# Moving the SBUF start addresses of split weights and moving activations in a two-block transformer kernel

## The chip, the core and the metric

The program runs on one core of one Trainium2 chip. The metric is the device time of one execution in microseconds (us); the time of a version is the median of its runs. In what follows PE is TensorE, PEld its weight loads, DVE is VectorE, ACT is ScalarE, POOL is GpSimd and SP is SyncE.

## The reference

Two transformer stages over 256 tokens of width 1024, all in fp32: a first block of two layers, then a second block of one layer.

```python
for l in range(2):                                  # first block
    h = rmsnorm(x, norm_mix[l]); proj = h @ w_in[l]
    # 12 slices: q, k, v, index heads, recurrence q/f/i/g, two gates
    y_attn = dsa_attention(...)                     # top-64 keys per query
    o = hgrn2_chunked(...)                          # gated linear recurrence
    merged = sigmoid(ga) * (y_attn @ w_proj_attn[l]) + sigmoid(gb) * (y_hgrn @ w_proj_hgrn[l])
    x = x + merged @ w_out[l]
    g, u = split(rmsnorm(x, norm_ffn[l]) @ w_ffn_in[l])
    x = x + (silu(g) * u) @ w_ffn_out[l]
...                                                 # second block: modulated norm, forgetting
                                                    # attention + depthwise conv, w_o, one more ffn
```

Nearly all the arithmetic is in the products with weights: 352 weight tiles of 128 x 1024 numbers.

## The kernel before

**Products in three parts.** Each weight tile arrives by DMA as fp32 in a tile `raw` (4 buffers). `do_split` (L720) makes two fp32r tiles of it: ACT writes the rounded half `wH`, DVE subtracts and writes the rest `wL` (6 buffers of 4096 bytes per partition for each). Activations are split in the same way into a high and a low tile. `mm3` (L781) then issues three matmuls for each product, and PE loads 128 columns of weights for each:

```python
PE.matmul(o, wH, xH, ...)      # stationary wH, moving xH
PE.matmul(o, wH, xL, ...)
PE.matmul(o, wL, xH, ...)
```

The first operand is the stationary one (loaded into the array), the second moves through it, 256 columns at a time. In what follows a "feature" matmul is one of these: stationary weights, 128 x 256 moving activations.

**The moving activations live in four kinds of tiles.** `xH`, `xL` (`act_pair`, L873) hold the normed input of a layer part; they feed `pair_mm` (L786), which is most of the kernel. `E` tiles hold the merged branches for `w_out`. The `t512` tiles (shown as `t` in the profile) hold the halves of the ffn's middle activation for `out_mm` (L896). The `b4` tiles (shown as `b`) hold the two branch outputs for `proj_mm` (L795). In the second block `token_mm`, `out_tm` and `first_tm` swap the roles: activations are stationary and 512 columns of `wH` or `wL` move. An output in PSUM is called `mm` or `side`.

**Where a tile starts.** A pool lays its buffers one behind another in every partition. `act_pair` makes its two tiles 128 elements longer than needed and starts the data `PLACE` = 28 elements (112 bytes) into them. `GAP` is a filler in the pool of constants, so that the pool of weights starts at a multiple of 512 bytes.

**What sets the order.** The program records every instruction, and `Recorder.issue` (L428) simulates the engines with estimated costs and emits the instructions in the order that it found. A `Buf` with a `tag` takes one of `bufs` places; which physical buffer it gets is left to the pool. In the first and second layer's ffn, runs of `pair_mm` matmuls alternate with runs of `out_mm` matmuls.

Of the kernel before, what the change touches and what calls it, by code (L numbers as in the profile page):

```python
# [15 lines left out]
F32 = mybir.dt.float32  # L16
F32R = mybir.dt.float32r
# [10 lines left out]
FF, NJ = 2816, 11  # L28
LINE = 128

GAP = 64

PLACE = 28
OUT_SHAPE = [256, 1024]
EPS = 1e-6
NEG = -1e30
# [208 lines left out]
class Buf:  # L245


    def __init__(self, pool, shape, dtype, name, tag, bufs, space):
        self.pool, self.shape, self.dtype, self.name, self.tag, self.bufs, self.space = pool, shape, dtype, name, tag, bufs, space
        n = int(np.prod(shape[1:]))  # L250
        self.writer = np.full(n, -1)
        self.readers = []
        self.group = [-1]
        self.ops = 0
        self.tile = None
        self.slot = None
        self.seq = None
        self.number = None
        self.read = {}

    def real(self):
        if self.tile is None:
            kw = {"tag": self.tag, "bufs": self.bufs} if self.tag else {}
            self.tile = self.pool.tile(self.shape, self.dtype, name=self.name, **kw)
        return self.tile
# [84 lines left out]
class Recorder:  # L350
# [77 lines left out]
    def issue(self):  # L428
# [25 lines left out]
        slots, waiting, first, line = {}, {}, {}, {}  # L454
        for op in ops:
            for b in op.bufs:
                if b.tag and b.seq is None:
                    slots.setdefault(b.tag, [0.0] * b.bufs)
                    b.seq = len(line.setdefault(b.tag, []))
                    line[b.tag].append(b)  # L460
                    first[b.tag] = 0
# [16 lines left out]
        while len(order) < len(ops):  # L478

            best = None  # L480
            for e in names:
                if avail[e]:
                    t = free_at[e]
                elif pending[e]:
                    t = max(free_at[e], pending[e][0][0])
# [6 lines left out]
            t, e = best  # L492
            while pending[e] and pending[e][0][0] <= t:
                _, _, op = heapq.heappop(pending[e])
                heapq.heappush(avail[e], (-op.urgency, op.index, op))
            op, skipped = None, []
            while avail[e]:
                item = max(avail[e], key=prio) if e in "VS" else avail[e][0]
                avail[e].remove(item)
                heapq.heapify(avail[e])  # L500
                cand = item[2]

                later, taken, turn = 0.0, {}, {}
                for b in sorted((b for b in cand.bufs if b.tag and b.slot is None), key=lambda b: b.seq):
                    s, n = slots[b.tag], taken.get(b.tag, 0)
                    f = turn.get(b.tag, first[b.tag])
                    jump = b.seq - f
                    ahead, reserve = JUMP.get(b.tag, (0, 0))
                    if len(s) <= n or (jump and (jump > ahead or len(s) - n <= reserve)):
                        later = None  # L510
                        waiting.setdefault(b.tag, []).append(cand)
                        break
                    later = max(later, sorted(s)[n])
                    taken[b.tag] = n + 1
                    if not jump:
                        f += 1
                        while f < len(line[b.tag]) and line[b.tag][f].slot:
                            f += 1
                        turn[b.tag] = f
                if later is not None:  # L520

                    for b in cand.bufs:
                        if b.space == "PSUM":
                            later = max([later] + [end + hop(x, e) for x, end in b.read.items() if x != e])
                            x = "S" if e == "V" else "V"
                            if e in "VS" and YIELD and free_at[x] <= t and any(
                                    p[0] <= t and p[2].urgency > cand.urgency and b in p[2].bufs for p in pending[x]):
                                later = max(later, t + 50.0)
                later = None if later is None else later if later > t else 0.0
                if later is None:  # L530
                    continue
                if later:
                    cand.ready = later
                    push(cand)
                    continue
                if e == "S" and TABLES.get(cand.func) and not (TABLES[cand.func] & tables):

                    other = [a for a in avail[e] if a[0] < item[0] + 4000.0 and (not TABLES.get(a[2].func) or TABLES[a[2].func] & tables)]
                    if other:
                        skipped.append(item)  # L540
                        continue
                op = cand
                break
# [29 lines left out]
            done = op.end + (LOAD_LATENCY if e == "DMA" else 0.0)  # L573
            order.append(op)
            for b in op.bufs:
                if b.space == "PSUM":
                    b.read[e] = op.end
                if b.tag and b.slot is None:
                    heapq.heappop(slots[b.tag])
                    b.slot = True  # L580
                    q, old = line[b.tag], first[b.tag]
                    while first[b.tag] < len(q) and q[first[b.tag]].slot:
                        first[b.tag] += 1
                    if first[b.tag] != old:
                        for w in waiting.pop(b.tag, []):
                            w.ready = max(w.ready, t)
                            push(w)
                if e == "PE" and b.number is not None:
                    at = max(at, b.number)
                b.ops -= 1  # L590
                if b.ops == 0 and b.tag:
                    heapq.heappush(slots[b.tag], done + 200.0)
                    for w in waiting.pop(b.tag, []):
                        w.ready = max(w.ready, done + 200.0)
                        push(w)
# [24 lines left out]
def program(tc, I, out, pw, cw, tap=None, stop=None):  # L620
# [11 lines left out]
    with es:  # L632
        es.enter_context(tc.manual_schedule())
        const = es.enter_context(tc.tile_pool(name="const", bufs=1))
        wp = es.enter_context(tc.tile_pool(name="wp", bufs=3))
        act = es.enter_context(tc.tile_pool(name="act", bufs=1))
# [4 lines left out]
        def body():  # L641
            uid = [0]

            def new(pool, shape, dt=F32, tag=None, bufs=None):
                n = int(np.prod(shape[1:]))
                line = LINE if dt == U8 else LINE // 4
                if pool is not psum and pool is not dram and n % line:

                    v = new(pool, [shape[0], -(-n // line) * line], dt, tag, bufs)[:, :n]
                    return v if len(shape) == 2 else v.rearrange("p (a b) -> p a b", a=shape[1])  # L650
                uid[0] += 1
                b = Buf(pool, shape, dt, f"{tag or 'c'}_{uid[0]}", tag, bufs or 1, "PSUM" if pool is psum else "SBUF")
                return View(b, np.arange(n).reshape([1] + list(shape[1:])), shape[0], ())
# [48 lines left out]
            NT = I["W"].shape[0]  # L702
            raw, split = {}, {}
            N_RAW, N_SPLIT = 4, 6

            halves = slice(0, 512), slice(512, 1024)

# [12 lines left out]
            def do_split(i):  # L720
                if i < NT and i not in split:
                    load(i)
                    H = new(wp, [128, 1024], F32R, tag="wH", bufs=N_SPLIT)
                    L = new(wp, [128, 1024], F32R, tag="wL", bufs=N_SPLIT)
                    R.feed = i
                    for c in cuts(i) if i < CUT or i not in HALVES else halves:
                        A(H[:, c], raw[i][:, c], AF.Copy)
                        tt(L[:, c], raw[i][:, c], H[:, c].bitcast(F32), OP.subtract)
                    R.feed, H.buf.number = None, i
                    split[i] = (H, L)  # L730

# [139 lines left out]
                return v, r, rstd  # L871

            def act_pair():  # L873
                return tuple(new(act, [128, 2048 + 128], F32R, tag=t, bufs=1)[:, PLACE:PLACE + 2048].rearrange("p (a b) -> p a b", a=8)
                             for t in ("xH", "xL"))

            def scaled_split(g, acc=None):

# [127 lines left out]
            def layer(l, first, X):  # L1006
                R.bias = NORM_BIAS if first else 0.0
                ms, rt, rstd = norm_x()
                R.bias = 0.0
                em, rtok = new(act, [128, 2], F32, tag="em"), new(act, [128, 2], F32, tag="rtok")  # L1010
                ts(em, ms, EPS, None, OP.mult)
                V.tensor_copy(rtok, rt)
                tap(f"rstd{l}", rstd)
# [45 lines left out]
                for t in range(2):  # L1059
                    n = 128 * (t + 1)  # L1060
# [27 lines left out]
                for p in range(2):  # L1088
# [12 lines left out]
                    if l == 1:  # L1101
                        for b in range(2):
                            h = 2 * p + b
                            s = slice(b * 256, b * 256 + 256)
# [39 lines left out]
                for c in range(4):  # L1144
                    for t in range(2):
                        o = (c % 2) * 256 + t * 128
# [65 lines left out]
                for lev in range(8):  # L1212
# [3 lines left out]
                    elif lev < 7:  # L1216
# [9 lines left out]
                        n = 64 // m  # L1226
                        for j in range(8):
                            t, h = divmod(j, 4)
                            for b in range(n):
                                o = h * 256 + t * 128 + 2 * m * b  # L1230
# [19 lines left out]
                    if lev < 6:  # L1250
                        n = 512 // m
                        o = 0 if lev == 0 else 512 - 2 * n
# [461 lines left out]
```

## Time and profile before

| what | value |
|---|---|
| time, median of 3 runs | 1131.16 us (1129.42 to 1132.87) |
| the profiled execution: its time, its span | 1129.97 us, 1128.2 us |
| PE busy, share of the span, matmuls | 1097.2 us, 97%, 9388 |
| PE weight loads busy | 1034.5 us, 92% |
| DVE busy | 857.5 us, 76% |
| ACT busy | 595.5 us, 53% |
| mean granted clock of PE | 0.992 of 2.4 GHz |

The span runs from the first to the last instruction in the trace. A matmul's duration in the trace is its latency (about 280 ns for a feature matmul), and consecutive matmuls overlap; how fast PE works is read from the distance between the starts of consecutive matmuls, called the pitch here.

### The profile page before, as it was taken

Reading aid. Unit: us, or ns where it says so; the run is one execution under the profiler, and the core shown is the slowest. Engines: PE = TensorE matmul, PEld = TensorE weight load, DVE = VectorE, ACT = ScalarE, POOL = GpSimd, SP = SyncE. Lnnn points to the kernel's source line nnn. Section 1 sums busy time; section 2 is a strip of 40 time slices with the busy share of each in tenths; the row PEclk is TensorE's granted clock in tenths of the full one; section 3 lists DMA queues with packets and bytes.
Section 4 is the critical chain, followed back from the end, with each engine's and each line's share of the span. In section 5 each row is a group of like instructions: output and inputs, shape, how many; then the busy total and the mean of one; then the engine's idle time right before and its main releaser. Section 6 shows DMA issues by size and latency. Waiting matters only on the chain.

```text
span 1128.2 us, 22970 instructions
## 1 busy us (share of the span) xinstructions
PE 1097.2 (97%) x9388; PEld 1034.5 (92%) x9388; DVE 857.5 (76%) x1590; ACT 595.5 (53%) x905; POOL 7.2 (1%) x16
## 2 busy tenths in 40 slices
PE   6999999999999999999999999999899989999996
PEld 6988999999999999888999999999798578999995
DVE  7999976899966589998676998756879668554554
ACT  6744694644444467446744544444754665443442
POOL 1000000000000000000000000000000000000000
PEclk9999999999999999999999999999999999999998
DMA  7553534689956543643345899655457225556550
GB/s 263 186 180 111 197 123 169 207 314 337 335 190 217 189 154 117 210 146 133 132 172 196 288 346 334 218 201 195 145 176 201 95 76 184 175 186 219 189 169 37
DMA packets 59992, 217.47 MB, mean 193 GB/s; under 512 B 6872, under 2 KB 10096, under 8 KB 56816
## 3 DMA queue, kind: packets, MB, share of 16 engines
q1 hardware_dynamic: 59888, 216.02, 55.8%
q8 instruction: 73, 1.20, 0.4%
q14 instruction: 31, 0.25, 0.1%
HBM read 214.19 MB, written 1.63 MB: 191 GB/s over the span
## 4 chain that ended last, share of the span: by engine, by line
PE 89%; DVE 6%; ACT 3%; issue 1%; DMA 1%; SPq 0%; DVEq 0%; ACTq 0%
PE mm L400 60%; PE side L400 29%; ACT t L400 2%; DVE t L400 1%; DVE b L400 1%; DVE wL L400 1%; DMA raw<-in_W 1%; DVE small L400 1%; ACT wH L400 1%; ACT L604 0%; DVE c L400 0%; DVE xL L400 0%; DVE AC L400 0%; SPq L400 0%; DVE sc L400 0%
## 5 line engine op out<-in xcount | busy, mean ns | idle before, releaser
L400 ACT ACTIVATE wH<-raw 128x1024 fp32r<-128x1024 f32 (+1 forms) x390 | 369.0, 968 | 400.5 <-PE mm L400 221.1
L400 DVE TENSOR_TENSOR wL<-raw,wH 128x1024 fp32r<-128x1024 f32 (+1 forms) x390 | 425.6, 1112 | 151.3 <-ACT wH L400 149.4
L400 PE MATMUL mm<-xH,wH 128*128 128x256 f32 x1760 | 486.8, 279 | 9.2 <-ACT wH L400 9.2
L400 PE MATMUL mm<-xH,wL 128*128 128x256 f32 x1760 | 488.3, 280 | 0.8 <-DVE wL L400 0.8
L400 PE MATMUL mm<-xL,wH 128*128 128x256 f32 x1760 | 488.5, 279 | 0.5 <-DVE xL L400 0.5
L400 PEld LDWEIGHTS mm<-xH,wH 128*128 128x128 f32 x1760 | 330.6, 189 | 11.7 <-ACT wH L400 9.2
L400 PEld LDWEIGHTS mm<-xL,wH 128*128 128x128 f32 x1760 | 331.2, 189 | 3.4 <-issue 0.9
L400 PEld LDWEIGHTS mm<-xH,wL 128*128 128x128 f32 x1760 | 330.8, 189 | 3.5 <-DVE wL L400 1.7
L400 PE MATMUL side<-t,wH 128*128 128x256 f32 x704 | 127.6, 281 | 0.0
L400 PEld LDWEIGHTS side<-t,wH 128*128 128x128 f32 x704 | 108.2, 188 | 0.0
L400 PE MATMUL side<-t,wL 128*128 128x256 f32 x352 | 98.8, 281 | 0.0
L400 ACT ACTIVATE t<-t 128x512 f32<-128x512 f32 (+2 forms) x80 | 48.9, 620 | 39.8 <-DVE t L400 37.0
L400 PEld LDWEIGHTS side<-t,wL 128*128 128x128 f32 x352 | 66.2, 188 | 0.0
L400 DVE SCALAR_TENSOR_TENSOR E<-E,b 128x1024 f32<-128x1024 f32 x48 | 57.9, 1221 | 4.1 <-DMA E<-in_ada 3.9
L400 PE MATMUL side<-wH,t 128*128 128x512 f32 x176 | 57.3, 394 | 0.0
L400 DVE TENSOR_TENSOR t<-t,t 128x512 f32<-128x512 f32 (+2 forms) x78 | 53.1, 681 | 3.7 <-ACT t L400 2.9
L400 PE MATMUL mm<-b,wH 128*128 128x256 f32 x256 | 46.6, 283 | 0.0
L400 PE MATMUL side<-E,wH 128*128 128x256 f32 x256 | 46.4, 281 | 0.0
L400 DVE TENSOR_TENSOR t<-mm,rstd 128x512 f32<-128x512 f32 (+1 forms) x50 | 33.7, 678 | 14.4 <-PE mm L400 14.1
L400 PE MATMUL mm<-wH,xH 128*128 128x512 f32 x96 | 38.7, 412 | 1.9 <-ACT xH L400 1.9
L400 PEld LDWEIGHTS mm<-b,wH 128*128 128x128 f32 x256 | 39.9, 191 | 0.0
L400 PEld LDWEIGHTS side<-E,wH 128*128 128x128 f32 x256 | 39.3, 188 | 0.0
(205 smaller groups left out, 1198.7 us busy)
## 6 DMA issues: line engine op xcount, KB each, us to landing
raw<-in_W SPq DMA_DIRECT2D x348, 512.0 KB, 4.3
E<-in_ada SPq DMA_DIRECT2D x24, 1024.0 KB, 7.0
b<-c SPq DMA_DIRECT2D x16, 128.0 KB, 4.6
c<-in_xT SPq DMA_DIRECT2D x4, 256.0 KB, 5.1
raw<-in_W SPq DMA_DIRECT2D x4, 256.0 KB, 4.9
b<-in_c SPq DMA_DIRECT2D x2, 512.0 KB
out_y<-E SPq DMA_DIRECT2D x4, 256.0 KB, 2.0
c<-E SPq DMA_DIRECT2D x4, 143.0 KB, 3.4
```

The costliest lines, as they stand in the source:

```text
L400: op.emit = lambda: getattr(real, method)(*[get(a) for a in args], **{k: get(a) for k, a in kw.items()})
```

## The change

The six buffers of `wH` become six places in one ring tile, and those of `wL` likewise. A place's number comes from the scheduler (`heappop(slots[...])[1]`) instead of from the pool, and the data starts 100 elements (400 bytes) into the ring. `act_pair` uses plain tiles that start at the tile's start. A filler of 96 elements (`GAP_E`, behind `em`) moves all tiles that are laid out behind it by 384 bytes.

```diff
-PLACE = 28
+PLACE = 100
+GAP, GAP_E = 64, 96
...
     def real(self):
+        if self.ring is not None:
+            n = int(np.prod(self.shape[1:]))
+            o = PLACE + self.slot * n
+            return self.ring.real()[:, o:o + n]
...
-                    slots.setdefault(b.tag, [0.0] * b.bufs)
+                    slots.setdefault(b.tag, [(0.0, k) for k in range(b.bufs)])
...
-                    heapq.heappop(slots[b.tag])
-                    b.slot = True
+                    b.slot = heapq.heappop(slots[b.tag])[1]
...
+            def ring(tag):
+                if tag not in rings:
+                    rings[tag] = Buf(wp, [128, N_SPLIT * 1024 + 128], F32R, f"{tag}_ring", f"{tag}_ring", 1, "SBUF")
+                uid[0] += 1
+                b = Buf(wp, [128, 1024], F32R, f"{tag}_{uid[0]}", tag, N_SPLIT, "SBUF", rings[tag])
+                return View(b, np.arange(1024).reshape(1, 1024), 128, ())
...
-                    H = new(wp, [128, 1024], F32R, tag="wH", bufs=N_SPLIT)
-                    L = new(wp, [128, 1024], F32R, tag="wL", bufs=N_SPLIT)
+                    H, L = ring("wH"), ring("wL")
...
-                return tuple(new(act, [128, 2048 + 128], F32R, tag=t, bufs=1)[:, PLACE:PLACE + 2048].rearrange("p (a b) -> p a b", a=8)
-                             for t in ("xH", "xL"))
+                return (new(act, [128, 8, 256], F32R, tag="xH", bufs=1), new(act, [128, 8, 256], F32R, tag="xL", bufs=1))
...
-                em, rtok = new(act, [128, 2], F32, tag="em"), new(act, [128, 2], F32, tag="rtok")
+                em, rtok = new(act, [128, 2 + GAP_E], F32, tag="em")[:, :2], new(act, [128, 2], F32, tag="rtok")
```

What the operands of the feature matmuls start at, as bytes past a multiple of 512 in a partition (every slice of 128 weight columns or 256 activation columns in a tile keeps the tile's value):

```text
tile                before   after     moving minus weights, modulo 512: before, after
wH, wL                   0     400
xH, xL  (pair_mm)      112       0     112   112
t512    (out_mm)       128       0     128   112
E       (w_out)        128       0     128   112
b4      (proj_mm)        0       0       0   112
```

On PE, at the place in the first layer's ffn where the first run of `out_mm` (moving `t512_526` and `t512_527`, output `side`) follows a run of `pair_mm` (moving `xH`, `xL`, output `mm`), there stood

```order
L400 MATMUL mm_536_3202<-xH_490_2951,wH_516_3129 128x256
L400 MATMUL mm_536_3202<-xL_491_2974,wH_516_3129 128x256
L400 MATMUL mm_536_3202<-xH_490_2951,wL_517_3156 128x256
L400 MATMUL side_504_3303<-t512_526_3217,wH_519_3144 128x256
L400 MATMUL side_504_3303<-t512_527_3229,wH_519_3144 128x256
L400 MATMUL side_504_3303<-t512_526_3217,wL_520_3189 128x256
```

and now stands

```order
L404 MATMUL mm_536_3060<-xH_490_2821,wH_ring_126 128x256
L404 MATMUL mm_536_3060<-xL_491_2844,wH_ring_126 128x256
L404 MATMUL mm_536_3060<-xH_490_2821,wL_ring_132 128x256
L404 MATMUL side_504_3156<-t512_526_3074,wH_ring_126 128x256
L404 MATMUL side_504_3156<-t512_527_3086,wH_ring_126 128x256
L404 MATMUL side_504_3156<-t512_526_3074,wL_ring_132 128x256
```

Nothing moved: the order of the instructions is the same on all five engines, and only the tiles' names and places differ.

On ACT, at weight tile 254 (the start of the second block, from which 38 tiles are split in two halves), the writes of `wH` with what each waits for (DMAHW is the landing of `raw`, PE the matmuls that read the place before) were

```order
L400 ACTIVATE wH_10042<-raw_9960 128x512 [waits DMAHW0_49,PE_49,Activation_49]
L400 ACTIVATE wH_10042<-raw_9960 128x512
L400 ACTIVATE wH_10090<-raw_9981 128x512 [waits DMAHW1_49,PE_49,Activation_49]
L400 ACTIVATE wH_10090<-raw_9981 128x512
L400 ACTIVATE wH_10117<-raw_10033 128x512 [waits DMAHW2_49,PE_49]
L400 ACTIVATE wH_10117<-raw_10033 128x512
```

and are

```order
L404 ACTIVATE wH_ring<-raw_9459 128x512 [waits DMAHW0_49,PE_49,Activation_49]
L404 ACTIVATE wH_ring<-raw_9459 128x512 [waits PE_49]
L404 ACTIVATE wH_ring<-raw_9479 128x512 [waits DMAHW1_49,PE_49,Activation_49]
L404 ACTIVATE wH_ring<-raw_9479 128x512 [waits PE_49]
L404 ACTIVATE wH_ring<-raw_9527 128x512 [waits DMAHW2_49]
L404 ACTIVATE wH_ring<-raw_9527 128x512 [waits PE_49]
```

Here a wait moved from the first half to the second: in a ring each half waits only for the matmuls that read that half. The second half waits for the same matmul that the whole tile waited for before, and the first half for one 12 to 24 matmuls earlier, or for none. For the tiles that are written in one piece the waits are unchanged.

## Rows read from the trace of the kernel before

**Rows 1.** The page, part 1: busy time of each engine.

```profile
PE 1097.2 (97%) x9388; PEld 1034.5 (92%) x9388; DVE 857.5 (76%) x1590; ACT 595.5 (53%) x905; POOL 7.2 (1%) x16
```

**Rows 2.** The page, part 4: the chain that ended last, by engine.

```profile
PE 89%; DVE 6%; ACT 3%; issue 1%; DMA 1%; SPq 0%; DVEq 0%; ACTq 0%
```

**Rows 3.** Waits of PE's matmuls: us in total, times, longest us.

```profile
PE mm L400 <- ACT wH L400: 9.2, 1, 9.2
...
PE mm L400 <- DVE wL L400: 0.8, 2, 0.5
```

**Rows 4.** Waits of all engines, same columns: the writes of the split weights.

```profile
ACT wH L400 <- PE mm L400: 221.1, 115, 5.3
...
ACT wH L400 <- DMA raw<-in_W: 36.9, 27, 5.9
```

**Rows 5.** Busy time by window, the two ffns of the first block.

```profile
core 0: us, PE busy (x) PEld busy (x) DVE busy (x) ACT busy (x) POOL busy (x), PEclk, DMA share, GB/s
245.00:407.00 162.00, 162.00 (x1399) 162.00 (x1399) 121.00 (x146) 73.66 (x83) 0.00 (x0) 1.00 0.72 254
643.00:813.00 170.00, 166.70 (x1437) 166.01 (x1435) 128.75 (x177) 79.64 (x99) 0.00 (x0) 1.00 0.71 249
```

**Rows 6.** Groups by line and form on PE: the feature matmuls and their counts.

```profile
L400 PE MATMUL mm<-xH,wH 128*128 128x256 f32 x1760 | 486.8, 279 | 9.2 <-ACT wH L400 9.2
L400 PE MATMUL side<-t,wH 128*128 128x256 f32 x704 | 127.6, 281 | 0.0
L400 PE MATMUL side<-t,wL 128*128 128x256 f32 x352 | 98.8, 281 | 0.0
L400 PE MATMUL mm<-b,wH 128*128 128x256 f32 x256 | 46.6, 283 | 0.0
L400 PE MATMUL side<-E,wH 128*128 128x256 f32 x256 | 46.4, 281 | 0.0
...
L400 PE MATMUL mm<-b,wL 128*128 128x256 f32 x128 | 36.0, 283 | 0.0
L400 PE MATMUL side<-E,wL 128*128 128x256 f32 x128 | 36.0, 281 | 0.0
```

**Rows 7.** Pieces of the chain that ended last: start us, us, what.

```profile
209.85 12.24 PE side L400 x103
...
365.70 3.08 PE side L400 x26
368.78 9.81 PE mm L400 x86
```

**Rows 8.** Timeline of PE: start us, us, what; starts at which the moving tile or the pitch changes.

```profile
170.69 0.28 PE L400 MATMUL mm<-b,wH 128*128 128x256 f32 x1
...
182.20 0.28 PE L400 MATMUL mm<-xL,wH 128*128 128x256 f32 x1
...
368.62 0.28 PE L400 MATMUL mm<-xH,wL 128*128 128x256 f32 x1
...
369.92 0.28 PE L400 MATMUL mm<-xL,wH 128*128 128x256 f32 x1
...
378.42 0.28 PE L400 MATMUL side<-t,wH 128*128 128x256 f32 x1
...
790.48 0.28 PE L400 MATMUL mm<-xL,wH 128*128 128x256 f32 x1
```

**Rows 9.** The same chain in the last ffn, where weights move, 512 columns each.

```profile
1040.55 2.78 PE side L400 x12
```

**Rows 10.** Groups by form on ACT: high halves written at 128 and 112 bytes past 512.

```profile
L400 ACT ACTIVATE t<-t 128x512 fp32r<-128x512 f32 x32 | 20.1, 628 | 27.4 <-DVE t L400 27.4
...
L400 ACT ACTIVATE xH<-t 128x512 fp32r<-128x512 f32 x8 | 5.0, 625 | 0.1
```

**Rows 11.** Groups by form on PE: fp32 transposes and matmuls of 128 columns.

```profile
L400 PE MATMUL side<-c,t 128*128 128x128 f32 x56 | 10.9, 277 | 0.2 <-DVE t L400 0.2
...
L400 PE MATMUL side<-c,c 128*128 128x128 f32 x32 | 4.2, 274 | 0.0
```

More of the change, by code (lines that the diff above doesn't have):

```diff
@@ L29 @@
 LINE = 128
-GAP = 64
-PLACE = 28
+GAP, GAP_E = 64, 96
+PLACE = 100
 OUT_SHAPE = [256, 1024]
@@ L245, with __init__ @@
 class Buf:
-    def __init__(self, pool, shape, dtype, name, tag, bufs, space):
-        self.pool, self.shape, self.dtype, self.name, self.tag, self.bufs, self.space = pool, shape, dtype, name, tag, bufs, space
+    def __init__(self, pool, shape, dtype, name, tag, bufs, space, ring=None):
+        self.ring, self.pool, self.shape, self.dtype, self.name, self.tag, self.bufs, self.space = ring, pool, shape, dtype, name, tag, bufs, space
         n = int(np.prod(shape[1:]))
@@ L512, in issue @@
                         break
-                    later = max(later, sorted(s)[n])
+                    later = max(later, sorted(s)[n][0])
                     taken[b.tag] = n + 1
@@ L516, in issue @@
                         f += 1
-                        while f < len(line[b.tag]) and line[b.tag][f].slot:
+                        while f < len(line[b.tag]) and line[b.tag][f].slot is not None:
                             f += 1
@@ L578, in issue @@
                 if b.tag and b.slot is None:
-                    heapq.heappop(slots[b.tag])
-                    b.slot = True
+                    b.slot = heapq.heappop(slots[b.tag])[1]
                     q, old = line[b.tag], first[b.tag]
-                    while first[b.tag] < len(q) and q[first[b.tag]].slot:
+                    while first[b.tag] < len(q) and q[first[b.tag]].slot is not None:
                         first[b.tag] += 1
@@ L591, in issue @@
                 if b.ops == 0 and b.tag:
-                    heapq.heappush(slots[b.tag], done + 200.0)
+                    heapq.heappush(slots[b.tag], (done + 200.0, b.slot))
                     for w in waiting.pop(b.tag, []):
@@ L704, in body @@
             N_RAW, N_SPLIT = 4, 6
+            rings = {}
+            def ring(tag):
[4 more added lines that the diff above has]
+                return View(b, np.arange(1024).reshape(1, 1024), 128, ())
             halves = slice(0, 512), slice(512, 1024)
```

## The prediction

> **What bounds the kernel now.** I read the engines' busy times first [rows 1], then the chain of work that ended last [rows 2], then PE's waits [rows 3]. PE is busy for 97% of the span, and 89% of the chain is PE's own matmuls. Its longest wait, 9.2 us, comes once, for the first weight tile; for `wL` it waits 0.8 us in all. The other side agrees: ACT's writes of `wH` waited 221.1 us for matmuls to free a place [rows 4], so the weights are ahead of PE. In the two ffns PE is busy 162.00 of 162 us and 166.70 of 170, while DVE has 121.00 and 128.75 us of work and ACT less, at a granted clock of 1.00, which is the 2.4 GHz level [rows 5]. So the kernel is as long as PE's stream of matmuls, and what matters is the pitch, from the start of one matmul to that of the next.
>
> The mean durations hide it: 279, 281 and 283 ns for the three kinds of moving tile [rows 6] are latencies of overlapping matmuls. I worked the pitch out from starts, for matmuls of one form (128 x 128 stationary, 128 x 256 moving, fp32r) that differ only in the tile they move:
> - moving `b4`, four `proj_mm` tiles of 24 matmuls each: from 170.69 to 182.20 us, 11.51 / 96 = **119.9 ns** [rows 8];
> - moving `E`: 12.24 / 103 = **118.8 ns** [rows 7];
> - moving `t512`: 3.08 / 26 = **118.5 ns** [rows 7];
> - moving `xH`, `xL`: 9.81 / 86 = **114.1 ns** [rows 7]. This last run falls in two [rows 8]: its first 11 matmuls, from 368.62 to 369.92 us, take 118.2 ns each, and the other 75, up to 378.42, 8.50 / 75 = **113.3 ns**. After a few slow matmuls the stream settles into a faster pace and keeps it; runs that move `t512` or `E` never settle, and `b4` settles at the slow pace.
>
> The four have PSUM, weights, clock and engine load in common, and the weights always start at a multiple of 512 bytes. What differs is the start of the moving tile: 0 for `b4`, 128 for `E` and `t512`, 112 for `xH` and `xL`. Beside each matmul PE loads the next weights (1034.5 us of loads beside 1097.2 us of matmuls [rows 1]), so two reads of SBUF always run together. My reading: they get in each other's way, and how much depends on the distance between the two addresses; at 112 there is a phase in which they don't collide.
>
> **The change, part by part.** It puts the weights at 400 and all four kinds of moving tiles at 0. Moving minus weights, modulo 512, becomes -400, which is 112, for every feature matmul. For `xH` and `xL` it was 112 already: both addresses shift together by 400. No instruction is added, removed or moved.
>
> *`t512`, `E` and `b4` settle like `xH`.* `t512` has 704 + 352 = 1056 matmuls, `E` 256 + 128 = 384, `b4` 384 [rows 6]. At 113.3 ns: 1056 x (118.5 - 113.3) = 5.5 us, 384 x (118.8 - 113.3) = 2.1 us, 384 x (119.9 - 113.3) = 2.5 us. Together 10.1 us.
>
> *`xH` runs behind them needn't settle anew.* In the four stretches where the kinds alternate, 52 runs of `xH`, `xL` follow directly on a run of another kind (the first at 182.20, the last at 790.48 us [rows 8]); 499 of their matmuls come before the pace settles, at most 11 in a run. If the pace survives the change of tile, as it survives changes of weight tile and PSUM bank within a run, they save 499 x (118.2 - 113.3) = 2.4 us. Each of the four stretches must settle once: 44 x 4.9 = 0.2 us lost. If the pace doesn't survive, the 2.4 us aren't saved, and `t512`, `E` and `b4` need about 11 matmuls of their own in each of as many runs: 52 x 11 x 5.3 = 3.0 us off the 10.1, and 7 are left. I take survival, since after the change nothing in the addresses tells the kinds apart: 10.1 + 2.4 - 0.2 = 12.3 us.
>
> *Matmuls that move weights.* In the last block activations are stationary and 512 columns of weights move: 2.78 / 12 = 231.7 ns [rows 9], or 2 x 115.9. Moving minus stationary goes from 384 to 400 where `t512` is stationary (264 matmuls) and stays 400 where `xH` is. I take nothing. Bounds: a best pace of 2 x 113.3 would save 264 x 5.1 = 1.3 us, the worst, 2 x 119.9, would cost 264 x 8.1 = 2.1 us.
>
> *fp32 matmuls.* `t512` and others move against the constants and `b4`. Two forms with stationary and moving tiles in different places last 277 and 274 ns [rows 11]. I take nothing, and allow this difference, 3 ns, on the some 350 fp32 matmuls that read a tile which moves: 1 us either way.
>
> *Writes at 400.* All 390 writes of `wH` and of `wL` go there instead of to 0. ACT's 128 x 512 copies took 625 ns into `xH` at 112 and 628 ns into `t512` at 128 [rows 10]: no price. Were there one, the weights' lead covers it: DVE has over 40 us to spare in each ffn [rows 5].
>
> *Waits of the ring.* Whole tiles wait for the same matmuls as before; first halves of 38 tiles may start earlier. As PE hardly waits for weights, the gain lies between nothing and the 0.8 us of waits for `wL` [rows 3]. I take nothing. Were the weights to fall behind, the next thing late would be `raw`: ACT waited 36.9 us for its landing [rows 4], and the DMA share in the ffns is already 0.72 [rows 5]; a PE 2% faster asks for 2% more.
>
> **Sum.** 12.3 us off PE's stream. The profiled execution took 1129.97 us, 1.2 below the median; 1129.97 - 12.3 = 1117.7, and against the median 1131.16 - 12.3 = 1118.9. I forecast 1119 us.
>
> **The rivals.**
> - *The pace is lost at each change of tile.* 7 us instead of 12.3: 1124 us. For it: every `xH` run behind another kind starts slow now, but it follows a run that was itself unsettled. Against it: 86 matmuls run across several weight tiles with one settling.
> - *Addresses don't matter*, and the pitches differ for some other reason that goes with the kinds of tiles, such as the alternation of outputs: 1131 us. Against it: `proj_mm` and `pair_mm` write the same `mm` banks with the same instructions and differ by 6.6 ns; `E` and `t512`, both at 128, agree within 0.3 ns in different layer parts. Beside it stands a rule of the Trainium skill. "SBUF — State Buffer", section "SBUF: two separate sides", says that on the engines' side only the port pair shared by VectorE and GpSimd causes contention and that TensorE waits for nobody, and "TensorE: Matmul & The Clock Gate", section "Step-by-step: what each phase is for", gives TensorE two independent read ports, one for each operand. By that rule no address changes a pitch and the time stays at 1131 us. The pitches of 113.3 and 119.9 ns in this trace disagree with it.
> - *The absolute start of the moving tile decides, not the distance* (the side of slower). Then `xH` and `xL` at 0 take the pace of `b4` at 0. They are 3 x 1760 = 5280 matmuls [rows 6]: 5280 x (119.9 - 114.1) = 30.6 us lost, and `t512` and `E` lose 1440 x 1.3 = 1.9 us more: 1131 + 32 = 1163 us; at the unsettled 118.5 ns, 23 us and 1154. It decides once the `xH` pitch rises by more than 12.3 / 5280 = 2.3 ns. For it: the weights never leave 0 in this trace, so start and distance vary together. Against it: in the last block the weights at 0 are what moves, and the pitch is 2 x 115.9, not 2 x 119.9 [rows 9]; the partner's address counts.
>
> **How the numbers follow.** Chances: 0.58 for the forecast, 0.20 for the pace lost at each change, 0.12 for no effect, 0.10 for the absolute start. About 0.3%, or 3.4 us, is what a measurement here can tell from no change. The first two cases are faster, so 0.78; same 0.12; slower 0.10. The low end is the forecast with the fp32 and the 512-column terms at their best (1.0 + 1.3) and the spread of the runs before (1.7 either way): 1119 - 4 = 1115, say 1114. The high end passes 1124 with the cost bounds on top (1.0 + 2.1) and some of the case of no effect: 1130. The rest of that case and the slower one stay outside. The likeliest case alone runs from 1114 to 1122.
>
> **What would show it.** In the profile after: runs that move `t512`, `E` and `b4` at 113.3 ns, 26 matmuls in 2.95 us where they took 3.08; `xH` runs in the ffns that start at that pace; `xH` runs after gaps as before. The two ffn windows are each some 3.6 us shorter. `t512` runs that begin with about 11 slow matmuls mean the first rival, pitches as now the second, an `xH` pitch above 116 ns the third. The forecast is also wrong if the pitch falls as said and the time doesn't: then PE's waits for `wL` or `raw` have grown.

## The result and the profile after

The changed kernel takes 1156.45 us (median of 6 runs, 1155.89 to 1158.04) where the kernel before, run beside it, takes 1130.8: ratio 1.0228, 95% interval 1.0215 to 1.0241. The prediction said 1119 us, 1114 to 1130, so it had the wrong sign.

The page of the kernel after, part 1 (busy time of each engine) and part 4 (the chain that ended last, by engine):

```profile
span 1154.9 us, 22990 instructions
...
PE 1125.4 (97%) x9388; PEld 1062.9 (92%) x9388; DVE 858.7 (74%) x1590; ACT 596.8 (52%) x905; POOL 7.2 (1%) x16
...
PE 94%; DVE 3%; ACT 2%; DMA 1%; issue 1%; SPq 0%; DVEq 0%; ACTq 0%
```

The same 9388 matmuls keep PE busy 28.2 us longer than in [rows 1]; DVE and ACT have about 1 us more. PE's share of the chain has risen from the 89% of [rows 2]. The next two fences show that PE doesn't wait more. First its waits (in total, times, longest us), then busy time by window for the stretches that begin and end with the matmuls of [rows 5]:

```profile
ACT wH_ring L404 <- PE mm L404: 232.9, 123, 5.5
...
PE mm L404 <- ACT wH_ring L404: 9.2, 1, 9.2
```

```profile
core 0: us, PE busy (x) PEld busy (x) DVE busy (x) ACT busy (x) POOL busy (x), PEclk, DMA share, GB/s
248.76:416.39 167.63, 167.63 (x1399) 167.63 (x1398) 120.75 (x145) 73.48 (x83) 0.00 (x0) 1.00 0.70 244
656.21:829.33 173.12, 172.11 (x1436) 171.66 (x1435) 126.08 (x172) 78.46 (x96) 0.00 (x0) 1.00 0.70 242
```

PE's only long wait is the old 9.2 us, and ACT waits for PE even longer than in [rows 4]. The granted clock is 1.00, the 2.4 GHz level, as before. In the first ffn PE is busy without a gap for 167.63 us where the same matmuls took 162.00. So every matmul simply comes later after the one before it. Pieces of the chain after (start us, us, what), the same stretches as in [rows 7]:

```profile
212.51 12.37 PE side L404 x103
...
373.84 3.12 PE side L404 x26
376.96 10.32 PE mm L404 x86
```

By pitch these are 120.1, 120.0 and 120.0 ns, where `E`, `t512` and `xH`, `xL` had 118.8, 118.5 and 114.1. Over all unbroken runs of 256-column matmuls the mean pitch of `xH` and `xL` went from 114.54 to 119.78 ns, of `t512` from 118.4 to 120.0, of `E` from 118.7 to 120.0, of `b4` from 119.78 to 120.0: 5080 x 5.24 + 1055 x 1.6 + 384 x 1.3 + 384 x 0.2 = 28.9 us. The profiled span grew by 1154.9 - 1128.2 = 26.7 us. Matched one by one, the 9388 matmuls of the two traces show where the rest went: the pauses (steps of over 135 ns, over 260 with 512 columns) are 2.9 us shorter in front of matmuls of `xH`, `xL` and small ones and 1.2 us longer among those of 512 columns. 26.6 of the 28.9 are `xH` and `xL`, the kinds for which I had said that nothing changes.

### The profile page after: what moved, and what is told of

It is laid out like the page before. It is cut to its first block, busy times and chain, and to the rows that moved or that the text cites. A ratio compares the mean times of both kernels' runs of the same rounds, so it can differ in the third digit from the quotient of the medians.

```text
span 1154.9 us, 22990 instructions
## 1 busy us (share of the span) xinstructions
PE 1125.4 (97%) x9388; PEld 1062.9 (92%) x9388; DVE 858.7 (74%) x1590; ACT 596.8 (52%) x905; POOL 7.2 (1%) x16
## 4 chain that ended last, share of the span: by engine, by line
PE 94%; DVE 3%; ACT 2%; DMA 1%; issue 1%; SPq 0%; DVEq 0%; ACTq 0%
PE mm L404 65%; PE side L404 29%; DMA raw<-in_W 1%; DVE wL_ring L404 1%; ACT t L404 1%; DVE small L404 1%; DVE t L404 1%; ACT wH_ring L404 1%; DVE xL L404 0%; SPq L404 0%; DVE b L404 0%; ACT L607 0%; DVE E L404 0%; DVEq L1721 0%; ACT xH L404 0%
## 5 line engine op out<-in xcount | busy, mean ns | idle before, releaser
L404 ACT ACTIVATE wH_ring<-raw 128x1024 fp32r<-128x1024 f32 (+1 forms) x390 | 369.8, 968 | 418.1 <-PE mm L404 232.9
L404 DVE TENSOR_TENSOR wL_ring<-raw,wH_ring 128x1024 fp32r<-128x1024 f32 (+1 forms) x390 | 426.1, 1111 | 164.6 <-ACT wH_ring L404 162.7
L404 PE MATMUL mm<-xH,wH_ring 128*128 128x256 f32 x1760 | 497.6, 285 | 9.2 <-ACT wH_ring L404 9.2
L404 PE MATMUL mm<-xL,wH_ring 128*128 128x256 f32 x1760 | 499.8, 286 | 0.4 <-DVE xL L404 0.4
L404 PE MATMUL mm<-xH,wL_ring 128*128 128x256 f32 x1760 | 499.8, 286 | 0.3 <-DVE wL_ring L404 0.3
L404 PEld LDWEIGHTS mm<-xH,wH_ring 128*128 128x128 f32 x1760 | 331.8, 189 | 11.6 <-ACT wH_ring L404 9.2
L404 PEld LDWEIGHTS mm<-xL,wH_ring 128*128 128x128 f32 x1760 | 332.7, 189 | 3.4 <-issue 0.9
L404 PEld LDWEIGHTS mm<-xH,wL_ring 128*128 128x128 f32 x1760 | 332.2, 189 | 2.9 <-DVE wL_ring L404 1.2
L404 PE MATMUL side<-t,wH_ring 128*128 128x256 f32 x704 | 129.3, 283 | 0.0
L404 PEld LDWEIGHTS side<-t,wH_ring 128*128 128x128 f32 x704 | 108.8, 188 | 0.0
```

What stands on the lines that cost most here:

```text
L404: op.emit = lambda: getattr(real, method)(*[get(a) for a in args], **{k: get(a) for k, a in kw.items()})
```

## The experiments

All but three are kernels that differ from the kernel after in starts alone (tE208 also in the lengths of some tiles). Each ratio is to runs of the kernel before beside that run. "(0, 400)" means moving tile at 0 and weights at 400 bytes past a multiple of 512.

| run | weights | `xH`, `xL` | `t512`, `E` | `b4` | median us | ratio to before (95%) | mean pitch of `xH`, `xL`, ns |
|---|---|---|---|---|---|---|---|
| before | 0 | 112 | 128 | 0 | 1130.8 | | 114.54 |
| after | 400 | 0 | 0 | 0 | 1156.45 | 1.0228 (1.0215 to 1.0241) | 119.78 |
| x112 | 400 | 112 | 0 | 0 | 1157.09 | 1.0234 (1.0219 to 1.0249) | 119.88 |
| w0 | 0 | 0 | 0 | 0 | 1155.24 | 1.0217 (1.0202 to 1.0232) | 119.85 |
| w0x112 | 0 | 112 | 0 | 0 | 1131.01 | 1.0004 (0.9995 to 1.0014) | 114.54 |
| w64 | 64 | 0 | 0 | 0 | 1134.06 | 1.0032 (1.0020 to 1.0044) | 116.06 |
| x80 | 400 | 80 | 0 | 0 | 1124.87 | 0.9948 (0.9934 to 0.9961) | 113.93 |
| w0m192 | 0 | 192 | 192 | 192 | 1132.32 | 1.0014 (1.0005 to 1.0023) | 116.12 |
| w32m224 | 32 | 224 | 224 | 224 | 1133.96 | 1.0032 (1.0021 to 1.0044) | 116.04 |
| tE208 | 16 | 208 | 208 | 0 | 1115.65 | 0.9865 (0.9848 to 0.9881) | 113.71 |

(tE208's starts are modulo 256.)

### Which of the two addresses: x112, w0, w0x112

x112 puts back the start of `xH` and `xL` alone, w0 that of the weights alone, w0x112 both:

```diff
-PLACE = 100
+PLACE = 0                      # w0 and w0x112
-return (new(act, [128, 8, 256], F32R, tag="xH", bufs=1), new(act, [128, 8, 256], F32R, tag="xL", bufs=1))
+return tuple(new(act, [128, 2048 + 128], F32R, tag=t, bufs=1)[:, 28:28 + 2048].rearrange("p (a b) -> p a b", a=8)
+             for t in ("xH", "xL"))      # x112 and w0x112
```

> The changed kernel with xH and xL back at 112 bytes past multiples of 512; the weights stay at 400 and t512, E and b4 at 0. If the start of the moving tile alone decides the pitch, xH and xL settle at 113.3 ns again and the others stay at the 120.0 ns that they show after the change: the time of before plus 1,440 matmuls of t512 and E at 1.5 ns more, about 1133 us. If the pair decides in some other way than by the distance modulo 512 (112 minus 400 is a new distance, 224), xH and xL stay above 116 ns: 1142 to 1156 us. If weights at 400 are what is slow, nothing is gained: 1156 us.

> The changed kernel with the ring's data at the ring's start: weights at 0 as before, all moving tiles at 0. If the start of the moving tile decides, nothing changes against the changed kernel: all four kinds at 120 ns, 1156 us. If weights at 400 are what is slow, xH and xL go back to 113 to 114 ns and the time to about 1131 us.

> The changed kernel with weights at 0 and xH, xL at 112, so that of the change only the ring and the tiles t512 and E at 0 are left. All theories that go by addresses give xH and xL 113.3 ns. The start of the moving tile adds 1.5 ns on 1,440 matmuls: 1133 us. If the ring with its places or its changed waits cost something by itself, the time is above 1135 us.

The run of 86 matmuls of `xH`, `xL` in the chain, in x112, w0 and w0x112 in this order:

```profile
377.05 10.32 PE mm L404 x86
```

```profile
377.02 10.32 PE mm L404 x86
```

```profile
368.46 9.80 PE mm L404 x86
```

With the moving tile back at 112 the pitch stays at 120.0 ns as long as the weights are at 400, and with the weights back at 0 it stays there as long as the moving tile is at 0. Of these pairs only (112, 0) gives the 9.8 us of before. So neither start decides alone. And w0x112, which keeps the rings, the order in which their places are handed out and all waits of the change, is as fast as before: these cost nothing that the measurement can tell, and the 25 us are the addresses. It came out 2 us below its 1133: `t512` and `E` did slow down, to 119.7 and 119.8 ns, but the 512-column matmuls whose stationary tile is `t512` got faster, from 232.2 to 228.7 ns, 0.9 us in sum.

### The table of pairs: sweep

PE alone runs, 48 matmuls `wH`, `wL` against `xH`, `xL` for each pair of starts:

```python
for s in (0, 25, 7, 8):                # weights start, in 16 bytes: 0, 400, 112, 128
    for m in range(32):                # moving start, in 16 bytes
        ...                            # two short fp32 matmuls
        for b in range(2):
            for k in range(8):
                mm3(ps[:, b * 256:b * 256 + 256], 4 * s + k * 128, 4 * m + k * 256, k == 0, k == 7)
```

> A program of its own that leaves out the whole computation and returns x: for each of 32 starts of the moving tile (0 to 496 bytes past a multiple of 512, by 16) and each of 4 starts of the weights (0, 400, 112, 128) it issues 48 feature matmuls in the kernel's pattern, with nothing running on the other engines. If the start of the moving tile alone decides, the pitch is the same function of it for all four starts of the weights: 120 ns at 0, near 118.5 at 128, 113.3 at 112 after some matmuls. If the distance decides, the four tables are shifted against each other by 400, 112 and 128 bytes. If other engines' traffic makes the difference, all pitches are equal here.

Pitch in ns over the last 24 matmuls; moving starts from 256 on repeat the first half, but for 4 of the 64 entries that differ by over 0.1 and by at most 1.5:

```
moving  weights 0   400     112     128
   0     120.00   120.00  120.04  120.00
  16     118.71   120.04  117.79  118.58
  32     116.67   119.92  118.71  118.54
  48     118.33   116.67  113.33  119.33
  64     117.79   118.79  117.75  113.33
  80     118.33   113.33  120.00  119.17
  96     120.00   123.33  118.33  118.33
 112     113.33   120.00  116.67  117.08
 128     118.83   118.33  120.00  120.00
 144     118.54   116.67  118.33  118.71
 160     117.42   120.00  120.00  116.67
 176     119.21   118.33  118.33  118.33
 192     113.33   116.67  117.96  117.79
 208     119.17   118.33  120.00  118.33
 224     118.33   118.17  120.00  120.00
 240     117.29   120.00  120.04  113.33
```

The timeline's groups show two of these runs, (112, 0) and (112, 400), by the first of each three matmuls (min/median/max latency in ns, first and last start in us): median latency 275 ns in the one and 283 in the other, and 5.2 and 5.5 us for 45 steps, with the same instructions, PSUM and clock. The first ten or so steps of (112, 0) are slow ones.

```profile
L44 PE MATMUL mhsa<-xH,wH x16: 275/275/363, 65.6 to 70.8; 128*128 128x256 f32 x16
```

```profile
L44 PE MATMUL mhsz<-xH,wH x16: 279/283/367, 261.1 to 266.6; 128*128 128x256 f32 x16
```

Three things follow. Nothing but PE was running, so the pitches of the kernel (113.3, 118.8, 120.0) are PE's own and need no traffic of other engines. The moving start counts modulo 256. And the distance of my prediction does not decide: distance 112 gives 113.33 ns at weights 0 and 120.00 at weights 400 (moving 0). A shift of both starts by 128 keeps the two good pairs, (112, 0) and (192, 0) become (240, 128) and (64, 128); a shift by 400 keeps only the second, as (80, 400), and takes (112, 0), the pair that the kernel used, to the 120.00 of (0, 400).

### What the table is worth in the kernel: x80 and w64

The table has one good pair for weights at 400: moving 80. x80 is x112 with 20 words in place of 28; w64 is the kernel after with `PLACE = 16`, all moving tiles left at 0.

> The changed kernel, weights at 400, with only xH and xL moved to 80, which is 400 minus 64 minus 256. By the rule of 64 bytes before the weights xH and xL settle at 113.3 ns and the rest stays at 120.0: 1133 us, although the distance modulo 512 (192) is not the 112 of before. If a start of 112 or 0 of the moving or the stationary tile is what counts, xH and xL stay slow: 1150 to 1157 us.

> The changed kernel with the ring's data 16 elements (64 bytes) into the ring instead of 100; all moving tiles stay at 0. In the sweep the pitch was 113.33 ns in all four tables at a moving start 64 bytes before the weights' start, modulo 256. If that is the rule, xH, xL, t512, E and b4 all settle at 113.3 ns here, and the pace survives the change of tile: the 12.3 us of the prediction come off the time before, about 1119 us. If the rule needs weights at a multiple of 128, or at 400 or 112, the pitch is between 116.7 and 120 and the time 1140 to 1156 us. If the kernel's other traffic breaks the pace after each change of tile: 1124 us.

The run of 86 in x80, then in w64:

```profile
367.21 9.76 PE mm L404 x86
```

```profile
370.42 10.13 PE mm L404 x86
```

x80 is 0.5% faster than before with the weights still at 400: the pair did it. It is also 8 us faster than the 1133 that I had expected. `t512`, `E` and `b4` ran at 118.3 ns and not at 120.0, at the same pair (0, 400) as in the kernel after; and where the stationary tile is `xH` and 512 columns of weights at 400 move, the pitch fell to 227.6 ns from the 233.9 that these matmuls had before, which is some 2 of the 6 us gained. w64, a pair inferred from a rule of distances (moving 64 bytes before the weights), is not slow and not good: 10.13 / 86 is 117.8 ns, and 1134 us is none of the times that I had named.

### More pairs, shorter loads: sweep_b

The same program with weights at 16, 32, ... 96, then with only 8 weight columns loaded, then with activations stationary and 512 columns of weights moving.

> A program of its own that leaves out the whole computation and returns x. First feature matmuls for weights at 16, 32, 48, 64, 80 and 96 and moving starts 0 to 240: the rule expects 113.3 ns at the moving start 64 before the weights' (modulo 256) in each of the six, and no other common distance; 112 past the weights only where the weights start at a multiple of 64. Then the same with only 8 weight columns loaded, weights at 0: if the pitch comes from the load of the next weights reading beside the moving tile, it is 113.3 ns for all moving starts; if the moving tile's start counts by itself, it follows the first table (120 at 0, 118.5 at 128, 113.3 at 112). Then 512 moving columns of weights over stationary activations at 0 and at 112: a pitch of 2 x 113.3 at some distance, and 231 to 233 ns at the distances that the kernels have had (400 and 384).

113.33 ns came at moving 208 for weights at 16; 144 and 224 for 32; 112 and 240 for 48; 176 for 64; 16 and 144 for 80; 208 for 96. In both sweeps together the distance of 112 is good for weights at 0, 32, 64, 96 and 128, and for none of 16, 48, 80, 112 and 400. A moving start 64 before the weights did better: 113.33 ns for eight of the ten weights starts, and 117.79 for the other two, (0, 64) and (32, 96). With 8 weight columns instead of 128 (weights at 0) 12 of 16 moving starts gave 113.33 ns, where two had; 0 gave 115.58, 192 rose to 116.67, and 32 and 160 gave 120.00, so neither of the two cases that I had named holds. The number of weight columns takes part in it; but a matmul with 8 weight columns also has only 8 rows of output, so that it is the load is not shown. With 512 moving columns the pitch ranged from 226.67 to 236.67 ns with the pair, 233.33 for most.

### All kinds at a good pair: w0m192, w32m224

A filler at the head of the activations' pool moves all four kinds of moving tile at once:

```diff
-PLACE = 100
+PLACE = 0                                                          # 8 in w32m224
             new(const, [128, GAP]).real()
+            Buf(act, [128, 48], F32, "fill", "fill", 1, "SBUF").real()   # 56 in w32m224
```

> The changed kernel with the rings' weights at 0 and, by a filler tile of 192 bytes at the head of the activations' pool, all four kinds of moving tile at 192, a pair of starts that ran at 113.33 ns in the sweep. Theory (the pair of starts sets the pitch, and a pace outlives a change of tile): all kinds settle at 113.3 ns and no run behind another kind settles anew. Then the terms of my prediction's sum come in at last, 10.1 + 2.4 - 0.2 = 12.3 us less than the kernel before: 1118.5 us, ratio 0.989. The matmuls that move 512 columns (648, stationary at 192, moving at 0) stand at a pair that no sweep measured: between 226.7 and 233.1 ns against 231.7 before, -3.2 to +0.9 us. First rival (the pace is lost at each change of tile): 7 us less than before, 1124. Second rival (the sweep's pairs don't carry over to a kernel that alternates tiles and banks, and the kernel's other work decides): t512, E and b4 stay at 118 ns or more, 1125 us or slower.

> As the run with weights at 0 and moving tiles at 192, but with weights at 32 and all moving tiles at 224: the same distance, 192, another residue of the weights modulo 128, and also a pair that ran at 113.33 ns in the second sweep. Theory: 1118.5 us, as there, but for the 512-column matmuls (stationary at 224, moving at 32, a pair that no sweep measured). The rivals give the same times as there. A difference between the two runs of more than 4 us would say that more than the pair of starts counts.

Both missed: 1132 and 1134 us instead of 1118.5, which is the time of the second rival (1125 or slower). Two pieces of the chain of w0m192, both runs at the pair (192, 0), the second from the long run at 561 us in which `xH`, `b4` and `E` alternate:

```profile
370.31 10.13 PE mm L404 x86
```

```profile
561.21 26.88 PE mm L404 x237
```

10.13 / 86 = 117.8 ns, 26.88 / 237 = 113.4. The pair has two paces. Both ffns (some 1500 matmuls each, through every change between `xH` and `t512`) ran at 117.8 from the first matmul to the last; the run of 524 from 561.2 us ran at 113.3 through `b4` and `E`. So a pace does outlive changes of tile, bank and weights, but here the one that the run fell into at its start.

### Does the entry choose the pace: entries

PE alone again; ten pairs, each entered in eight ways:

```python
if entry < 6:      # one matmul of 64 + 32 * entry columns at the same pair
    PE.matmul(ps[:, 0:64 + 32 * entry], wH[:, w0:w0 + 128], xH[:, x0:x0 + 64 + 32 * entry], ...)
else:              # eight of 256 columns with the moving tile at 128 or 0, weights at 0
    ...
...                # then the 48 matmuls at the pair
```

> A program of its own that computes nothing of the reference (it hands the input back): no engine but PE works. Ten pairs of starts (moving, weights), each run eight times as 48 fp32r matmuls of 128 x 128 by 128 x 256; before each run stand two short fp32 matmuls and an entry: one matmul of 64, 96, 128, 160, 192 or 224 columns at the same pair, or eight of 256 columns at the pair (128, 0) or (0, 0). Theory (a pair has one or more steady paces, and the moment at which a run comes in chooses among them; where the kernel with 192 against 0 ran some stretches at 113.3 ns and some at 117.8, both are steady): (192, 0) and (224, 32) end at 113.3 after some entries and at 117.8 after others; (112, 0), (80, 400) and its shift (208, 16) end at 113.3 after every entry, as the matmuls of xH did in the kernel in every long run; (0, 0), (0, 400) and (112, 400) end at 120.0 after every or nearly every entry and never at 113.3. Rival (the pair alone sets the pitch, and the two paces in the kernel come from the other engines' traffic): every pair ends at one pitch whatever the entry, 113.3 for (112, 0), (192, 0), (224, 32), (80, 400), (208, 16).

Pitch in ns over the last 24 matmuls, one column for each entry:

```
(112, 0)    113.33 113.33 113.33 113.33 113.33 113.33 113.33 113.33
(192, 0)    113.33 113.33 113.33 117.79 113.33 113.33 113.33 113.33
(224, 32)   113.33 117.75 113.33 117.75 113.33 117.75 113.33 117.75
(0, 0)      119.96 120.00 120.00 120.00 120.00 120.00 120.00 120.00
(128, 0)    120.00 118.54 118.54 118.83 118.83 120.00 120.00 118.62
(80, 400)   113.33 113.33 113.33 113.33 113.33 113.33 113.33 113.33
(208, 16)   113.33 113.33 113.33 113.33 113.33 113.33 113.33 113.33
(0, 400)    120.00 118.33 118.33 118.33 118.33 118.33 120.00 118.33
(112, 400)  120.00 120.00 120.00 120.00 120.00 120.00 120.00 120.00
(0, 64)     113.33 113.33 113.33 117.75 113.33 117.75 117.75 117.75
```

Two entries of (192, 0), 64 and 160 columns, as pieces of the chain (each with one longer step at its head, 203 and 156 ns):

```profile
73.08 5.53 PE pbea L59 x48
...
91.15 5.69 PE pbed L59 x48
```

With nothing else running the same pair ends at 113.33 or at 117.8 ns by its entry, so two paces need no traffic of other engines. Each entry ran once; that the same entry gives the same pace again is not shown. (112, 0), (80, 400) and (208, 16) reach 113.33 from every entry; (0, 0) and (112, 400) end at 120. (0, 64) has both paces, which settles w64, whose mean of 116.06 is a mixture: its stretches run at 113.3 or at 117.8. It also leaves the distance of 64 before the weights with a pace of 113.33 at nine of the ten weights starts; the tenth, (32, 96), was entered in one way only. I missed (0, 400): 118.33 after six entries of eight, not 120. In the kernels it had both as well, 120.0 after the change and 118.3 in x80.

### A kernel with what was learnt: tE208

(208, 16) is (80, 400) with both starts 384 lower, and takes less room.

```diff
-PLACE = 100
+PLACE, MOVE = 4, 52
...
+            def mov_at(pool, n, dt, tag, bufs):
+                return new(pool, [128, n + 64], dt, tag=tag, bufs=bufs)[:, MOVE:MOVE + n]
...
-                return new(tmp, [128, 512], dt, tag="t512", bufs=9)
+                return mov_at(tmp, 512, dt, "t512", 9)
...
-                return (new(act, [128, 8, 256], F32R, tag="xH", bufs=1), new(act, [128, 8, 256], F32R, tag="xL", bufs=1))
+                return tuple(mov_at(act, 2048, F32R, t, 1).rearrange("p (a b) -> p a b", a=8) for t in ("xH", "xL"))
...
-                mH, mL = (new(act, [128, 8, 256], F32R, tag="E", bufs=2) for _ in range(2))
+                mH, mL = (mov_at(act, 2048, F32R, "E", 2).rearrange("p (a b) -> p a b", a=8) for _ in range(2))
...
```

> The changed kernel with the rings' weights at 16 modulo 256 and xH, xL, t512 and E all at 208 (each tile 256 bytes longer, three small constants in one tile and em and rtok in one, to make room); b4 stays at 0, for which there is no room. (208, 16) is (80, 400) with both starts 384 lower, and 400 with 80 was the pair at which xH reached 113.3 ns in every long run. Theory: xH, xL, t512 and E keep 113.3 ns through each other's runs, b4 takes 118.3 as (0, 16) did in the sweep. Against the run with only xH and xL at 80 (1124.9 us) t512 and E save 1056 x 5.0 + 384 x 5.0 = 7.2 us and xH in the two ffns needs no settling behind t512, some 2 us more; the 512-column matmuls whose stationary tile is t512 go to the pair of xH, 176 + 88 by up to 6 ns = 1.5 us: 1115 us, between 1114 and 1118, ratio about 0.986 to the kernel before. Rival (a pair that is good by itself is lost at each change of tile): t512 and E save less than half of it, 1121 or more.

1115.65 us, 1.35% faster than before and as forecast. Its windows from and to the matmuls of [rows 5], and a run of `t512` and the run of 86 in the chain:

```profile
242.81:401.17 158.36, 158.36 (x1400) 158.36 (x1399) 120.34 (x146) 73.47 (x82) 0.00 (x0) 1.00 0.74 259
635.09:798.90 163.81, 162.79 (x1437) 162.34 (x1435) 126.67 (x172) 78.26 (x96) 0.00 (x0) 1.00 0.74 256
```

```profile
360.95 2.95 PE side L402 x26
363.90 9.75 PE mm L402 x86
```

The 26 matmuls that move `t512` take 2.95 us, the very figure that my prediction gave as the sign of its success, and the `xH` run behind them is at 113.4 ns from its first matmul. Against before, the first ffn is 162.00 - 158.36 = 3.6 us shorter, also as predicted, and the second has 166.70 - 162.79 = 3.9 us less of busy PE. `t512` fell to 113.36 ns, `E` to 113.61, `xH`, `xL` to 113.71 over all runs: 5.3 + 2.0 + 4.2 us, 0.5 for `b4`, and some 3 us from the 512-column matmuls, now at 227.5 to 227.8 ns.

## Why the prediction was wrong

- **The bound and the measure held.** PE's stream sets the time, PE waits for the weights no more than before, and the pitch from starts explains the result, while mean latencies (285 ns after, 279 before) only hint at it.
- **The step that failed** is the reading under "what bounds the kernel", that the collision "depends on the distance between the two addresses", and with it the line of the change that for `xH` and `xL` "both addresses shift together by 400", at no cost. The sweep puts (112, 0) at 113.33 and (0, 400) at 120.00. It failed because in the trace of before the weights always start at 0: three pitches for three moving starts fit a function of the distance as well as one of either start or of the pair. I wrote that sentence down as an argument for a rival and not against my own reading. The distance of 112 turned out good at every weights start measured that is a multiple of 32, and 400 is none. A distance of 64 before the weights has a pace of 113.33 at nine of ten weights starts, but at (0, 64), (192, 0) and (224, 32) 117.8 beside it: not even there does the distance alone set the pitch.
- **The 10.1 us for `t512`, `E`, `b4`** came out with the other sign: +1.7, +0.5 and +0.1 us, since (0, 400) has no pace of 113.3. At a pair that has it the sizes were right (tE208, for `t512` and `E`).
- **That the pace survives a change of tile** was right, against the first rival: in tE208 `t512` and `xH` keep 113.3 through each other's runs. But it carries a slow pace just as far: after the change 120.0 holds through every kind, and in w0m192 117.8 through two ffns.
- **The small terms** held. 512-column matmuls: 233.0 ns after, 233.9 (`xH` stationary) and 232.2 (`t512`) before, nothing in sum. Writes at 400: ACT's copies into `wH` have a mean of 968 ns before and after. Ring, places and waits: w0x112 at 1.0004.
- **The rivals.** That addresses don't matter is refuted by the sweep: with nothing else running, the same instructions take 113.33 or 120.00 ns by their starts. The Trainium skill ("TensorE: Matmul & The Clock Gate", section "Step-by-step: what each phase is for") gives TensorE two independent read ports; the sweep disagrees with what I drew from it, that no address changes a pitch, and does not show whether it is the two reads that get in each other's way. That the absolute start of the moving tile decides gave the right time, 1154 to 1163 us, but its mechanism is refuted: x112 has the old moving start and is as slow. It had the right size because both it and the truth take `xH` and `xL` to the pace of `b4`. That both starts count was no case of mine, and my 0.10 for slower was too low for a change that moves all of them.

**What stays open.** What collides within a matmul is not shown: why the period is 256 bytes, why 128 for both together, and what makes one pair fall to 113.33 from every entry and another not. The run with 8 weight columns says that their number takes part, not how, nor whether by the load.

## What to carry to other kernels

Where PE is the bound and streams matmuls back to back, work out the pitch from starts and compare kinds of tiles that differ in address only; a difference of 6 ns in 113 is 5% of the stream. Place weights and moving tiles as a pair, and measure the pair by itself, from several entries, before building it in: a rule read off one kernel in which one of the two never moves is not a rule. Prefer a pair that reaches its fast pace from every entry, since a stream keeps a slow pace as stubbornly as a fast one.

## What the runs showed of the hardware

- For fp32r matmuls of 128 x 128 by 128 x 256 the steady pitch depends on both start addresses: 113.33 to 123.33 ns. Most pairs end on 113.33, 116.67, 118.33, 120.00 or 123.33 ns; at 2.4 GHz 113.33, 116.67, 120.00 and 123.33 are 272, 280, 288 and 296 clock periods. None of the 160 pairs (ten weights starts, 16 moving starts modulo 256) ended below 113.33.
- Some pairs have two steady paces: (192, 0), (224, 32) and (0, 64) 113.33 and 117.8, (0, 400) 118.33 and 120.00. Which one a run took changed with its entry, and it kept that pace over changes of tile, bank and weights.
- With 512 moving columns it is 226.67 to 236.67 ns by the pair (32 pairs, stationary tile at 0 or 112).
